# Expert weights with neighbouring rows in a partition: one 8 KB run in place of four or two rows, in a two-layer encoder with a mixture of experts

## The chip, the cores and the metric

The kernel runs on one core of a Trainium2 chip. The metric is the time of one execution on the device in microseconds (us). A profile is one execution, recorded by the hardware profiler. The engines are TensorE (PE for matmuls, PEld for its weight loads), VectorE (DVE), ScalarE (ACT), GpSimd (POOL) and SyncE (SP, which here only starts DMAs). A DMA moves data between HBM and the core's on-chip memory (SBUF); a matmul's result lies in PSUM.

## What is computed

Two layers of an encoder with 512 tokens of width 1024. Each has a mixer (attention and two kinds of linear recurrence), a mixture of 16 experts, and a gated embedding. The change touches the experts alone:

```python
h = rms_norm(x, norm_ffn_g[i])
# each token picks one of 4 groups, and 2 of the 4 experts in it, with weights comb[t, e]
for e in range(N_EXPERTS):                            # 16
    a = jax.nn.silu(t @ w_gate[e]) * (t @ w_up[e])    # [1024, 512] each
    y = y + comb[:, e:e + 1] * (a @ w_down[e])        # [512, 1024]
x = x + y
```

All of it is float32. The weights of one expert are 6 MB, those of a layer's experts 96 MB.

## The kernel before

The function `moe` computes a layer's experts one after another. On the chip a table is made of which tokens go to which expert, and the experts are ranked by how many tokens they have. The experts 0 and 1 are done first, whatever their rank; for the others the number of the expert is known only at run time, and SP reads it from SBUF (`fetch`) before it can start that expert's weight loads. In this order the first ten experts (class `Expert`, here called wide) have room for 112 rows, the last six (class `Small`, narrow) for 64. Wide experts split each weight into two parts, `hi` on ScalarE (line 244) and `lo` on VectorE (line 297), and do three matmuls for each product; narrow experts use float32 matmuls directly and do no split.

The steps for expert e are these:

- `fetch` (line 1676 and after) builds the expert's object and calls `gather` (line 1491), which clears a place in `XE` with a GpSimd memset (the first two places are filled once on ScalarE, line 1312) and gathers the expert's rows from DRAM with an indirect DMA on GpSimd's queue. `XE` has two places, used in turn, and gathers run two experts ahead.
- `scale` (line 1507) multiplies the gathered rows by the norm's gain on VectorE, in place. It is done for wide experts; narrow ones multiply by `gc`, the gain by columns, while they copy the transposed rows from PSUM (line 1605).
- `x_T` transposes the rows on TensorE in blocks of 128 columns; `x_split` copies them to SBUF.
- `gate_up(0..7)` loads the gate and up weights, 1 MB in one DMA (a block of 4 of the 8 row blocks), and does the matmuls. Row k*128 + p of a weight lies in partition p as its block k (`"(k p) n -> p k n"`), so a partition gets rows that lie 128 rows apart in DRAM.
- `silu` (ScalarE, line 1551) and `times` (VectorE, line 1554 for wide, line 1621 for narrow) make the activation `a`, 512 columns; `a_T` transposes it, `a_split` splits it.
- `down(0..3)` loads the down weights, 1 MB in one DMA (2 of the 4 row blocks), and does the matmuls. `store` (line 1591) copies the result and scatters the rows to DRAM with an indirect DMA on GpSimd's queue.

The main loop (from line 1696) weaves neighbouring experts: in the turn of e, the gate and up parts of e, the transposes of e+1, then the down parts of e-1; `store` of e-2 stands near the start. The weight loads of a layer go through a ring of 16 buffers of 1 MB (`e8`), in the order of use, on SP's queue; a load can start when the buffer's last reader is done. The tile framework puts the instructions of each engine in one fixed order at build time; `order(a, b)` asks it to keep b behind a.

Of the kernel before, what the change touches and what calls it, by code (L numbers as in the profile page):

```python
# [22 lines left out]
D = 1024  # L23
# [43 lines left out]
def tile_encoder(ctx: ExitStack, tc: tile.TileContext, A, out):  # L67
# [502 lines left out]
    def mixers(l, T_):  # L570
# [652 lines left out]
        def router_weights():  # L1223
            nonlocal wr3, wrs3, rb

            wr = small("wr", 160, bufs=1)
            wr3 = r3(wr, 8)
            nc.scalar.dma_start(wr3[:, :, 0:4], A["w_group"][l].rearrange("(k p) n -> p k n", p=128))
            nc.scalar.dma_start(wr3[:, :, 4:20], A["w_router"][l].rearrange("(k p) n -> p k n", p=128))
            gc = small("gc", 8, bufs=1)  # L1230
            nc.scalar.dma_start(gc, A["norm_ffn_g"][l].rearrange("(k p) -> p k", p=128))
            g.tensor_tensor(wr3, wr3, bc(gc.unsqueeze(2), [128, 8, 20]), OP.mult)
            st["gc"] = gc
            wrs = small("wrs", 320, F32R, bufs=1)
            wrs3 = r3(wrs, 8)
            hilo(wrs3[:, :, 0:20], wrs3[:, :, 20:40], wr3)
            rb = small("rb", 20, bufs=1)
            nc.scalar.dma_start(rb[:, 0:4], A["b_group"][l].partition_broadcast(128))
            nc.scalar.dma_start(rb[:, 4:20], A["b_router"][l].partition_broadcast(128))
# [59 lines left out]
    def moe(l, X, rsx, lg3):  # L1299
# [3 lines left out]
        st["first"], st["n"], st["h"], st["sc"] = None, 0, 0, None  # L1303
        gB = gain(A["norm_ffn_g"][l], D, "gain")

        wv_ = A["w_expert_gate"][l, 0].rearrange("(k p) n -> p k n", p=128)
        W0 = r3(t8("W0"), 4)
        nc.sync.dma_start(W0, wv_[:, 0:4, :])
        XE = t8("XE")
        i = st["last"]  # L1310
        for n in range(2):
            order(i, act(XE[:, n * D:n * D + D], bc(one_t, [128, D]), AF.Copy, scale=0.0))


        def sm4(name, n):
# [172 lines left out]

        YE = []

        def gather(ixc, n, m=CAP):
            xe = XE[0:m, (n % 2) * D:(n % 2) * D + D]
            if n > 1 or m > CAP:
                if n == 2 and Z2:
                    act(xe, bc(one_t[0:m], [m, D]), AF.Copy, scale=0.0)
                else:
                    g.memset(xe, 0.0)
            st["got"] = g.indirect_dma_start(out=xe, out_offset=None, in_=xd[:, :],
                                             in_offset=bass.IndirectOffsetOnAxis(ap=ixc[0:m], axis=0),
                                             bounds_check=T - 1, oob_is_err=False)  # L1500
            if n > G2:
                order(st["parts"], st["got"])
            if n == 2:
                st["sc"] = st["got"]
            return xe

        def scale(xe, m=CAP, after=None):
            i = v.tensor_tensor(xe, xe, gB[0:m], OP.mult)
            if after is not None:
                order(after, i)  # L1510

        class Expert:


            def __init__(self, n, w_, xe, iyc, rsc, m=CAP):
                self.n, self.w, self.xe, self.iyc, self.rsc, self.m = n, w_, xe, iyc[0:m], rsc[0:m], m
                self.rd = {}

            def x_T(self):
# [14 lines left out]
            def gate_up(self, i):  # L1534

                c, u = i // 4, i % 4
                if u == 0:
                    self.pg = mm() if c == 0 else self.pg
                    self.pu = mm() if c else None
                ps = (self.pu if c else self.pg)[0:self.m]  # L1540
                if u % 2 == 0:
                    wv_ = self.w(("w_expert_gate", "w_expert_up")[c]).rearrange("(k p) n -> p k n", p=128)
                    self.rw = W0 if self.n == c == u == 0 else load(wv_[:, 2 * u:2 * u + 4, :])
                hi, lo = split(self.rw[:, u % 2 * 2:u % 2 * 2 + 2, :], "g" if self.n == 0 and (c, u) in GS0 else "a")
                for j in range(2):
                    k = 2 * u + j
                    mm3(ps, self.xh[:, k, :], self.xl[:, k, :], hi[:, j, :], lo[:, j, :], k == 0, k == KD - 1)

            def silu(self):
                self.a = t2("a")[0:self.m]  # L1550
                act(self.a, self.pg[0:self.m], AF.Silu, scale=self.rsc)

            def times(self):
                v.tensor_tensor(self.a, self.pu[0:self.m], self.a, OP.mult)

            def a_T(self):
                self.pa = tp()
# [5 lines left out]
                self.i = hilo(self.ah, self.al, r3(self.pa, 4)[:, :, 0:self.m])  # L1563

            def load_down(self, k):
                wv_ = self.w("w_expert_down").rearrange("(k p) n -> p k n", p=128)
                raw = load(wv_[:, k:k + 2, :])
                self.rd[k], self.rd[k + 1] = raw[:, 0:1, :], raw[:, 1:2, :]

# [24 lines left out]
        class Small(Expert):  # L1594
# [7 lines left out]
            def x_split(self, q):  # L1602
                if q == 0:
                    self.x = r3(t8("xhl")[:, 0:512], 8)
                    v.tensor_tensor(self.x, r3(self.ps, 8), bc(st["gc"].unsqueeze(2), [128, 8, 64]), OP.mult)  # L1605

            def gate_up(self, k):

                if k == 0:
                    self.pg = mm()  # L1610
                if k % 4 == 0:
                    self.rw = [load(self.w(nm).rearrange("(k p) n -> p k n", p=128)[:, k:k + 4, :]) for nm in ("w_expert_gate", "w_expert_up")]
                for c in range(2):
                    pe.matmul(self.pg[64 * c:64 * c + 64], self.x[:, k, :], self.rw[c][:, k % 4, :], start=(k == 0), stop=(k == KD - 1))  # L1614

            def silu(self):
                self.a = t2("a")[64:128]
                self.si = act(self.a, self.pg[0:64], AF.Silu, scale=self.rsc)

            def times(self):  # L1620
                v.tensor_tensor(self.a, self.pg[64:128], self.a, OP.mult)

            def a_T(self):
                self.pa = tp()
# [54 lines left out]
        def fetch(e):  # L1679
# [8 lines left out]
            EX.append((Expert if e < NBIG else Small)(e, w_, gather(ic, e, m), iys[:, e:e + 1], rps[:, e:e + 1], m))  # L1688

        for e in range(GA):  # L1690
            fetch(e)
        scale(EX[0].xe)
        EX[0].x_T()
        EX[0].x_split(0)
        EX[0].x_split(1)
        for e in range(16):
            cur = EX[e]
            prev = EX[e - 1] if e else None
            if e == 15:
                s0 = turn[0]  # L1700
            fetch(e + GA)
            cur.gate_up(0)
            cur.gate_up(1)
            if e > 1:
                EX[e - 2].store()
            if e < NBIG - 1:
                scale(EX[e + 1].xe, after=st["lo"] if e else None)
            if e == 0:
                by_slot(rps, to_parts(V2, OH))
            cur.gate_up(2)  # L1710
# [2 lines left out]
            cur.gate_up(3)  # L1713
            if prev:
                prev.a_split()
            for u in range(4):
                cur.gate_up(4 + u)
                if u == (1 if e < NBIG else 3):
                    cur.silu()
                if e == 0 and u == EU:  # L1720
# [55 lines left out]
        with tc.If(cnt > 0):  # L1776
            with tc.For_i(0, 4) as r_:
# [6 lines left out]
                with tc.For_i(0, 16) as e_:  # L1784
# [3 lines left out]
                    with tc.If(ce > 0):  # L1788
# [5 lines left out]
                        ex = Expert(16, w_, gather(ic, 0, 128), jc, rc_, 128)  # L1794
                        scale(ex.xe, 128)
                        ex.x_T()
                        for q in range(2):
                            ex.x_split(q)
# [147 lines left out]
```

## Time and profile before

| what | us |
|---|---|
| median of 3 runs | 1418.15 (1415.32 to 1418.39) |
| the profiled execution | 1418.6 |
| its span, first to last instruction | 1416.9 |
| TensorE busy | 1318.4 (93%) |
| VectorE busy | 1018.7 (72%) |
| ScalarE busy | 816.7 (58%) |
| GpSimd busy | 290.7 (21%) |

304.34 MB are moved in 170,080 packets. The profile's busy time counts work that overlaps, and the end of a matmul is modelled: where TensorE's matmuls follow each other without a gap, it is read as "no idle time", not as a rate. A timeline line shows when an instruction (or a merged group of them) starts, how long it takes, its engine, line, tiles, and in brackets how long its engine was idle before and what ended that. The page's slices cut the span into 40 equal parts.

### The profile page before, as it was taken

The page shows a single profiled execution, that of the slowest core. Times are in us where ns is not written, and L with a number is a line of the kernel's source. Part 1 is how long each engine was busy: PE and PEld are TensorE (multiplying, and loading weights), DVE is VectorE, ACT ScalarE, POOL GpSimd, SP SyncE. Part 2 cuts the span into 40 slices and gives each one's busy share as a digit, 9 for nine tenths or more (in the row PEclk, how much of TensorE's full clock was granted, in tenths as well). Part 3 has the DMA queues.
Part 4 walks back from the last instruction along what each step waited for, and adds up shares of the span by engine and source line. Part 5 has one row for each costly group of instructions (what it writes and reads, how often), then busy time and mean ns, then how long its engine had stood idle before and what let it go on. Part 6 is the DMA issues. An engine that isn't in the chain of part 4 may idle for free. (4 is left out here: it accounts for less than half of the span.)

```text
span 1416.9 us, 23046 instructions
## 1 busy us (share of the span) xinstructions
PE 1318.4 (93%) x8180; PEld 1024.5 (72%) x8180; DVE 1018.7 (72%) x1931; ACT 816.7 (58%) x1565; POOL 290.7 (21%) x362
## 2 busy tenths in 40 slices
PE   6998999999899999878989989999989999998797
PEld 5787878898577775227967878789966777742296
DVE  5769887567999994118666788874779999921285
ACT  6554566554688883116555536755556888821364
POOL 4124000110344422102011330002104344221000
PEclk9999999999899999999989999999999999999999
DMA  6221224554899999998143111336358999999871
GB/s 169 80 88 49 72 60 112 187 163 162 263 376 367 369 364 365 366 379 303 35 128 91 58 46 60 79 94 226 125 208 291 382 378 371 363 358 380 318 247 60
DMA packets 170080, 304.34 MB, mean 215 GB/s; under 512 B 29216, under 2 KB 68164, under 8 KB 169956
## 3 DMA queue, kind: packets, MB, share of 16 engines
q1 hardware_dynamic: 143712, 280.00, 57.1%
q0 software_dynamic: 7872, 18.99, 4.0%
q10 hardware_dynamic: 18372, 3.79, 1.4%
q8 instruction: 67, 1.10, 0.3%
q14 instruction: 57, 0.47, 0.1%
HBM read 283.54 MB, written 20.77 MB: 215 GB/s over the span
## 5 line engine op out<-in xcount | busy, mean ns | idle before, releaser
L297 DVE TENSOR_TENSOR lo<-we,hi 128x1024 fp32r<-128x1024 f32 x236 | 276.7, 1219 | 5.9 <-ACT hi L244 2.0
L244 ACT ACTIVATE hi<-we 128x1024 fp32r<-128x1024 f32 x236 | 246.0, 1059 | 47.6 <-PE mm L335 24.6
L486 PE MATMUL zb<-hi,Th 128*128 128x256 f32 x576 | 169.4, 295 | 0.0
L487 PE MATMUL zb<-lo,Th 128*128 128x256 f32 x576 | 163.1, 283 | 0.0
L488 PE MATMUL zb<-hi,Tl 128*128 128x256 f32 x576 | 162.6, 282 | 0.0
L1591 POOL DMA_INDIRECT yd<-YE,iys x32 | 87.8, 2745 | 181.3 <-ACT YE L244 173.1
L1614 PE MATMUL mm<-we,xhl 128*64 128x512 f32 x384 | 95.7, 599 | 22.6 <-DMA we<-in_w_expert_up_dram 21.3
L486 PEld LDWEIGHTS zb<-hi,Th 128*128 128x128 f32 x576 | 109.0, 190 | 8.9 <-issue 8.0
L333 PE MATMUL mm<-hi,xhl 128*112 128x512 f32 x288 | 114.2, 398 | 0.6 <-issue 0.6
L334 PE MATMUL mm<-lo,xhl 128*112 128x512 f32 x288 | 113.6, 394 | 0.0
L335 PE MATMUL mm<-hi,xhl 128*112 128x512 f32 x288 | 113.2, 393 | 0.0
L487 PEld LDWEIGHTS zb<-lo,Th 128*128 128x128 f32 x576 | 109.3, 190 | 2.9 <-issue 1.7
L488 PEld LDWEIGHTS zb<-hi,Tl 128*128 128x128 f32 x576 | 108.9, 189 | 1.6 <-issue 1.3
L297 DVE TENSOR_TENSOR lo<-w,hi 128x1024 fp32r<-128x1024 f32 (+3 forms) x66 | 73.8, 1119 | 24.4 <-PE zb L487 18.6
L244 ACT ACTIVATE hi<-w 128x1024 fp32r<-128x1024 f32 (+3 forms) x66 | 63.0, 955 | 42.3 <-PE zb L488 35.9
L1614 PEld LDWEIGHTS mm<-we,xhl 128*64 128x64 f32 x384 | 27.6, 136 | 82.2 <-issue 43.2
L244 ACT ACTIVATE a<-mm,rps 112x512 f32<-112x512 f32 (+1 forms) x32 | 21.9, 686 | 96.1 <-PE mm L1614 78.3
L1605 DVE TENSOR_TENSOR xhl<-tp,gc 128x512 f32<-128x512 f32 x12 | 8.3, 690 | 81.5 <-PE mm L1614 55.2
L244 ACT ACTIVATE P<-mm,nm 128x512 f32<-128x512 f32 x64 | 44.1, 689 | 39.5 <-DVE nm L1016 39.2
L486 PE MATMUL zb<-hi,mh 128*128 128x256 f32 x224 | 65.0, 290 | 1.4 <-DVE X L1138 1.4
L244 ACT ACTIVATE YE<-zb 112x512 f32<-112x512 f32 (+1 forms) x62 | 34.7, 589 | 50.9 <-PE zb L1640 37.1
L333 PE MATMUL zb<-hi,ah 128*112 128x512 f32 x160 | 64.0, 402 | 0.0
(455 smaller groups left out, 3472.7 us busy)
## 6 DMA issues: line engine op xcount, KB each, us to landing
we<-in_w_expert_up_dram SPq DMA_DIRECT2D x64, 1024.0 KB, 16.8
we<-in_w_expert_down_dram SPq DMA_DIRECT2D x64, 1024.0 KB, 15.6
we<-in_w_expert_gate_dram SPq DMA_DIRECT2D x62, 1024.0 KB, 17.1
w<-in_w_in_dram SPq DMA_DIRECT2D x44, 512.0 KB, 3.8
we<-in_w_ple_gate_dram SPq DMA_DIRECT2D x8, 1024.0 KB, 13.6
Y<-yd SPq DMA_DIRECT2D x16, 512.0 KB, 9.1
X<-xd SPq DMA_DIRECT2D x12, 512.0 KB, 9.1
w<-in_w_out_dram SPq DMA_DIRECT2D x10, 512.0 KB, 3.8
```

Source lines behind the costliest of these rows:

```text
L244: i = s.activation(out_, in_, func, **kw)
L297: i = (g if eng == "g" else v).tensor_tensor(l3, src, h3.bitcast(F32), OP.subtract)
L333: i = pe.matmul(ps, ah, bh, start=start, stop=False)
L334: pe.matmul(ps, ah, bl, start=False, stop=False)
L335: return i, pe.matmul(ps, al, bh, start=False, stop=stop)
L486: pe.matmul(pt[tb], ah[c][:, sl], hi, start=(k == 0 and (by_tb or tb % 2 == 0)), stop=False, skip_group_check=True)
L487: pe.matmul(pt[tb], ah[c][:, sl], lo, start=False, stop=False, skip_group_check=True)
L488: pe.matmul(pt[tb], al[c][:, sl], hi, start=False, stop=(k == nk - 1), skip_group_check=True)
L1591: st["sc"] = g.indirect_dma_start(out=yv[self.n], out_offset=bass.IndirectOffsetOnAxis(ap=self.iyc, axis=0), in_=ye, in_offset=None, bound ...
L1605: v.tensor_tensor(self.x, r3(self.ps, 8), bc(st["gc"].unsqueeze(2), [128, 8, 64]), OP.mult)
L1614: pe.matmul(self.pg[64 * c:64 * c + 64], self.x[:, k, :], self.rw[c][:, k % 4, :], start=(k == 0), stop=(k == KD - 1))
```

## The change

The experts' weights are read with `"(p k) n -> p k n"`: partition p gets the neighbouring rows 8p to 8p+7 (gate and up, of which a load takes 4) or 4p to 4p+3 (down, of which a load takes 2), so a load's 8 KB for a partition lie in one run in DRAM. The matmuls must then meet the columns of x and of `a` in the same order: `scale` writes the gathered rows permuted into the second half of `XE`, and `silu` and `times` write `a` permuted. `XE` has one place for gathered rows and one for scaled rows; `scale` is now done for all experts, the multiplication by `gc` is gone, and the clears of gathered places are gone but for one fill at the start. In the loop the gather for e+2 stands behind `scale` of e+1.

```diff
-        wv_ = A["w_expert_gate"][l, 0].rearrange("(k p) n -> p k n", p=128)
+        wv_ = A["w_expert_gate"][l, 0].rearrange("(p k) n -> p k n", p=128)
...
-        for n in range(2):
-            order(i, act(XE[:, n * D:n * D + D], bc(one_t, [128, D]), AF.Copy, scale=0.0))
+        order(st["last"], act(XE[:, 0:D], bc(one_t, [128, D]), AF.Copy, scale=0.0))
...
         def gather(ixc, n, m=CAP):
-            xe = XE[0:m, (n % 2) * D:(n % 2) * D + D]
-            if n > 1 or m > CAP:
-                if n == 2 and Z2:
-                    act(xe, bc(one_t[0:m], [m, D]), AF.Copy, scale=0.0)
-                else:
-                    g.memset(xe, 0.0)
-            st["got"] = g.indirect_dma_start(out=xe, out_offset=None, in_=xd[:, :],
+            st["got"] = g.indirect_dma_start(out=XE[0:m, 0:D], out_offset=None, in_=xd[:, :],
...
-        def scale(xe, m=CAP, after=None):
-            i = v.tensor_tensor(xe, xe, gB[0:m], OP.mult)
+        def scale(m=CAP, after=None):
+            i = v.tensor_tensor(XE[0:m, D:2 * D].rearrange("t (k p) -> t p k", k=8), XE[0:m, 0:D].rearrange("t (p k) -> t p k", k=8),
+                                gB[0:m].rearrange("t (p k) -> t p k", k=8), OP.mult)
             if after is not None:
                 order(after, i)
 
+        def quad(ap):
+            return ap.rearrange("t (p k) -> t p k", k=4)
+
+        def by4(ap):
+            return ap.rearrange("t (k p) -> t p k", k=4)
...
-                    wv_ = self.w(("w_expert_gate", "w_expert_up")[c]).rearrange("(k p) n -> p k n", p=128)
+                    wv_ = self.w(("w_expert_gate", "w_expert_up")[c]).rearrange("(p k) n -> p k n", p=128)
...
-                act(self.a, self.pg[0:self.m], AF.Silu, scale=self.rsc)
+                act(by4(self.a), quad(self.pg[0:self.m]), AF.Silu, scale=self.rsc)
...
-                v.tensor_tensor(self.a, self.pu[0:self.m], self.a, OP.mult)
+                v.tensor_tensor(by4(self.a), quad(self.pu[0:self.m]), by4(self.a), OP.mult)
...
-                wv_ = self.w("w_expert_down").rearrange("(k p) n -> p k n", p=128)
+                wv_ = self.w("w_expert_down").rearrange("(p k) n -> p k n", p=128)
...
-                    v.tensor_tensor(self.x, r3(self.ps, 8), bc(st["gc"].unsqueeze(2), [128, 8, 64]), OP.mult)
+                    v.tensor_copy(self.x, r3(self.ps, 8))
...
-        for e in range(GA):
-            fetch(e)
-        scale(EX[0].xe)
+        fetch(0)
+        scale()
+        fetch(1)
...
-            fetch(e + GA)
             cur.gate_up(0)
             cur.gate_up(1)
             if e > 1:
                 EX[e - 2].store()
-            if e < NBIG - 1:
-                scale(EX[e + 1].xe, after=st["lo"] if e else None)
+            if 0 < e < NBIG:
+                scale(EX[e + 1].m, st["lo"])
+                fetch(e + GA)
...
             if prev:
                 prev.a_split()
+            if NBIG <= e < 15:
+                scale(CAPS, prev.i[1])
+                fetch(e + GA)
             for u in range(4):
                 cur.gate_up(4 + u)
+                if e == u == 0:
+                    scale(CAP, st["lo"])
+                    fetch(GA)
```

The narrow experts' gate and up loads, `silu` and `times` change in the same way as the wide ones'.

## Rows read from the trace of the kernel before

**Rows 1.** The page: its span, and the DMA's busy tenths in 40 slices.

```profile
span 1416.9 us, 23046 instructions
...
DMA  6221224554899999998143111336358999999871
```

**Rows 2.** Windows, layer one: start:end, length, busy PE, PEld, DVE, ACT, POOL; clock; DMA share; GB/s.

```profile
440.00:520.00 80.00, 80.00 (x385) 61.95 (x384) 77.93 (x77) 68.97 (x83) 33.16 (x14) 1.00 1.02 366
...
580.00:636.00 56.00, 43.27 (x185) 13.40 (x182) 5.07 (x9) 7.01 (x12) 4.12 (x5) 1.00 1.04 380
```

**Rows 3.** Waits in 584 to 636 us: waiter, releaser, us in total, times, longest.

```profile
PEld mm L1614 <- DMA we<-in_w_expert_up_dram: 14.0, 5, 3.1
```

**Rows 4.** TensorE's timeline: starts of narrow experts, and the ends, both layers.

```profile
556.47 2.80 PE L1614 MATMUL mm<-we,xhl 128*64 128x512 f32 x12
...
568.15 2.75 PE L1614 MATMUL mm<-we,xhl 128*64 128x512 f32 x12
...
614.54 1.07 PE L1614 MATMUL mm<-we,xhl 128*64 128x512 f32 x2 [0.22 <-DMA we<-in_w_expert_gate_dram]
...
634.04 1.94 PE L1640 MATMUL zb<-we,aT 128*64 128x512 f32 x8 [0.97 <-DMA we<-in_w_expert_down_dram]
635.91 1.09 PE L1655 MATMUL tp<-ident,p 128*128 128x128 f32 x8
...
1269.62 2.75 PE L1614 MATMUL mm<-we,xhl 128*64 128x512 f32 x12
...
1335.27 1.09 PE L1655 MATMUL tp<-ident,p 128*128 128x128 f32 x8
```

**Rows 5.** GpSimd's timeline: the scatters of two neighbouring wide experts.

```profile
455.15 5.41 POOL L1591 DMA_INDIRECT yd<-YE,iys  x1 [4.20 <-ACT YE L244]
...
472.78 5.43 POOL L1591 DMA_INDIRECT yd<-YE,iys  x1 [4.17 <-ACT YE L244]
```

**Rows 6.** Groups of VectorE by form: busy us, mean ns of one, idle before.

```profile
L1508 DVE TENSOR_TENSOR XE<-XE,gain 112x1024 f32<-112x1024 f32 x20 | 24.4, 1221 | 0.7 <-DMA XE<-xd,ix 0.7
...
L1554 DVE TENSOR_TENSOR a<-mm,a 112x512 f32<-112x512 f32 x20 | 13.6, 682 | 0.0
...
L966 DVE COPY kvs<-mm 64x256 f32<-64x256 f32 x8 | 3.3, 412 | 3.9 <-PE mm L955 3.9
...
L1630 DVE COPY aT<-tp 128x256 f32<-128x256 f32 x12 | 5.1, 425 | 28.5 <-PE tp L1626 16.1 <-issue 12.4
...
L637 DVE CAST wsh<-wst 128x256 fp32r<-128x256 f32 x2 | 1.2, 588 | 0.3 <-DMA wst<-in_w_in_dram 0.3
...
L972 DVE TENSOR_TENSOR_SCAN Ss<-db,kvs 64x512 f32<-64x512 f32 x8 | 10.1, 1266 | 0.1
```

**Rows 7.** Queue q1 in stretches of 3 us (from 1361, 1295, 333, 625): packets, MB, share.

```profile
q1 hardware_dynamic: 1036, 1.04, 109.1%
...
q1 hardware_dynamic: 573, 1.14, 104.3%
...
q1 hardware_dynamic: 328, 1.28, 104.1%
...
q1 hardware_dynamic: 286, 1.12, 102.4%
```

**Rows 8.** Head of the stage: timelines, and us to landing (360 to 400, 440 to 520).

```profile
367.31 1.01 SPq L265 DMA_DIRECT2D we<-in_w_expert_gate_dram  x2
...
371.41 1.70 POOL L1498 DMA_INDIRECT XE<-xd,ixs  x1 [2.63 <-PE mm L1407]
...
375.05 3.48 DVE L297 TENSOR_TENSOR lo<-we,hi 128x1024 fp32r<-128x1024 f32 x3
...
384.67 1.21 DVE L1508 TENSOR_TENSOR XE<-XE,gain 112x1024 f32<-112x1024 f32 x1
...
XE<-xd,ixs POOLq DMA_INDIRECT x3, 10.6
...
XE<-xd,ixs POOLq DMA_INDIRECT x4, 8.0
```

More of the change, by code (lines that the diff above doesn't have):

```diff
@@ L1232, in router_weights @@
             g.tensor_tensor(wr3, wr3, bc(gc.unsqueeze(2), [128, 8, 20]), OP.mult)
-            st["gc"] = gc
             wrs = small("wrs", 320, F32R, bufs=1)
@@ L1309, in moe @@
         XE = t8("XE")
-        i = st["last"]
-        for n in range(2):
-            order(i, act(XE[:, n * D:n * D + D], bc(one_t, [128, D]), AF.Copy, scale=0.0))
+        order(st["last"], act(XE[:, 0:D], bc(one_t, [128, D]), AF.Copy, scale=0.0))
         def sm4(name, n):
@@ L1504, in gather, with __init__ @@
                 st["sc"] = st["got"]
-            return xe
-        def scale(xe, m=CAP, after=None):
-            i = v.tensor_tensor(xe, xe, gB[0:m], OP.mult)
+        def scale(m=CAP, after=None):
+            i = v.tensor_tensor(XE[0:m, D:2 * D].rearrange("t (k p) -> t p k", k=8), XE[0:m, 0:D].rearrange("t (p k) -> t p k", k=8),
+                                gB[0:m].rearrange("t (p k) -> t p k", k=8), OP.mult)
             if after is not None:
                 order(after, i)
+        def quad(ap):
+            return ap.rearrange("t (p k) -> t p k", k=4)
+        def by4(ap):
+            return ap.rearrange("t (k p) -> t p k", k=4)
         class Expert:
-            def __init__(self, n, w_, xe, iyc, rsc, m=CAP):
-                self.n, self.w, self.xe, self.iyc, self.rsc, self.m = n, w_, xe, iyc[0:m], rsc[0:m], m
+            def __init__(self, n, w_, ixc, iyc, rsc, m=CAP):
+                self.n, self.w, self.ixc, self.iyc, self.rsc, self.m = n, w_, ixc, iyc[0:m], rsc[0:m], m
+                self.xe = XE[0:m, D:2 * D]
                 self.rd = {}
@@ L1611, in gate_up @@
                 if k % 4 == 0:
-                    self.rw = [load(self.w(nm).rearrange("(k p) n -> p k n", p=128)[:, k:k + 4, :]) for nm in ("w_expert_gate", "w_expert_up")]
+                    self.rw = [load(self.w(nm).rearrange("(p k) n -> p k n", p=128)[:, k:k + 4, :]) for nm in ("w_expert_gate", "w_expert_up")]
                 for c in range(2):
@@ L1617, in silu @@
                 self.a = t2("a")[64:128]
-                self.si = act(self.a, self.pg[0:64], AF.Silu, scale=self.rsc)
+                self.si = act(by4(self.a), quad(self.pg[0:64]), AF.Silu, scale=self.rsc)
             def times(self):
-                v.tensor_tensor(self.a, self.pg[64:128], self.a, OP.mult)
+                v.tensor_tensor(by4(self.a), quad(self.pg[64:128]), by4(self.a), OP.mult)
             def a_T(self):
@@ L1687, in fetch @@
                 w_ = lambda nm: A[nm][l][bass.DynSlice(pv, 1)].rearrange("o k n -> (o k) n")
-            EX.append((Expert if e < NBIG else Small)(e, w_, gather(ic, e, m), iys[:, e:e + 1], rps[:, e:e + 1], m))
-        for e in range(GA):
-            fetch(e)
-        scale(EX[0].xe)
+            EX.append((Expert if e < NBIG else Small)(e, w_, ic, iys[:, e:e + 1], rps[:, e:e + 1], m))
+            gather(ic, e, m)
+        fetch(0)
+        scale()
+        fetch(1)
         EX[0].x_T()
@@ L1793, in moe @@
                         w_ = lambda nm: A[nm][l][bass.DynSlice(e_, 1)].rearrange("o k n -> (o k) n")
-                        ex = Expert(16, w_, gather(ic, 0, 128), jc, rc_, 128)
-                        scale(ex.xe, 128)
+                        ex = Expert(16, w_, ic, jc, rc_, 128)
+                        gather(ic, 0, 128)
+                        scale(128)
                         ex.x_T()
```

## The prediction

> **What bounds the kernel now.** I read the page's slices first, then busy time by stage, then the timelines of TensorE, VectorE and GpSimd in the expert stage. The slices [rows 1] show two long stretches with the DMA engines full: the expert stages of the two layers, from about 367 us (the first load that needs a run-time expert number, [rows 8]) to about 636 us, and 701.5 us later again. The change lies only there.
>
> A full DMA doesn't yet say that DMA sets the end. In 440 to 520 us [rows 2] TensorE has no idle time and VectorE has 2.07 us of 80; the DMA is full because 16 buffers let it run ahead. In 580 to 636 us TensorE is idle for 12.7 of 56 us, and its waits name expert loads [rows 3]. So there are two parts: the ten wide experts run at the engines' pace and draw on the stock of buffers; when the stock is gone, in the four last narrow experts, loads set the pace.
>
> How much that costs is read from TensorE's starts [rows 4]. A narrow expert without a wait takes 568.15 - 556.47 = 11.68 us. The 16th expert would then start at 568.15 + 3 x 11.68 = 603.2 and end after 11.68 + 2 x 1.94 us, at 618.8; it ended at 635.9. In the second layer 1269.62 + 35.0 + 15.6 = 1320.2 against 1335.3. So there are 17.1 and 15.1 us that faster loads can give at most, 32 in all; beyond that the engines' chain is the end.
>
> **Part 1, the pieces.** Per partition a load now takes 4 rows of 2 KB that lie 256 KB apart (gate, up) or 2 rows of 4 KB (down); after it, 8 KB in one run. From stretches with pieces of one size [rows 7], engine time for 8 KB is share x 16 engines x 3 us / MB x 8192 B: 413 ns in 1 KB pieces, 360 ns in 2 KB, and in 4 KB 320 ns in one stretch and 360 in another. With a fixed price f per piece, 1 to 2 KB gives f = 13 ns (53/4), 2 to 4 KB gives 20 (40/2) or 0. No row shows 8 KB on this queue. I take f = 10, the middle of 0 and 20. Gate and up then save 3f = 30 ns per 8 KB, down saves 10. After 367 us a layer issues 56 gate and up loads and 28 down loads (14 experts x 6) of 128 such pieces over 16 engines: 56 x 8 x 30 + 28 x 8 x 10 ns = 15.7 us (0 to 31). The loads for the first two experts lie in stretches where the DMA has gaps, and give nothing. The loads would then allow ends at 620.2 and 1319.6.
>
> [...]
>
> **Part 2, the permuted stores on VectorE.** `scale` (112x1024, 1.22 us) and `times` (112x512, 0.68 us) [rows 6] now store each element 512 B from the one before, and `times` also reads so. VectorE's bounds: the copy at L966 reads PSUM in 512 B steps and costs 412 ns for 256 columns against 425 for a plain copy: 0 per element. The slow cast at L637 stores into SBUF in rows 512 B apart (32 words in each) and costs 588 ns for 256 columns, 163 more: 0.64 ns per element. I take 0.64, because that one hops in an SBUF store, as the change does. Then `scale` is 0.66 us longer and `times` 0.33, 0.98 us per wide expert. Per expert of 17.63 us [rows 5] VectorE is idle for 2.07/80 x 17.63 = 0.46 us [rows 2]. TensorE has no idle time and VectorE takes over as the slower: 0.98 - 0.46 + 0.2 (half of the small idle stays) = 0.72 us per expert, ten experts, 7.2 us per layer later into the narrow ones. Bounds: 0 to 15, from a scan that costs 1266 ns for 512 columns, 1.14 ns per element over `times` [rows 6]: (1.17 + 0.58 - 0.46 + 0.2) x 10.
>
> [...]
>
> **Part 3, one buffer for gathered rows.** Before, gathers ran two experts ahead in two places. Now rows are gathered into one half and scaled into the other, so the gather for expert e+2 waits for `scale` of e+1, and that waits for the transposes of e. In the steady part this has cover: from one `scale` to the next are 17.6 us, and the gather takes 5.4 us behind the scatter on GpSimd's queue [rows 5], 1.7 to issue and 8.0 to land [rows 8]: 15.1, with 2.5 us left. With narrow experts the 11.7 us hold 9.7 of issue and landing and leave 2 for the scatter. At the head the cover is thin: the gather for expert 2 was issued at 371.4 and its rows scaled at 384.7 [rows 8]; now it waits for `scale` of expert 1, which stands behind the fifth weight split (the second of the three that start at 375.1, [rows 8]) and ends near 380, and lands 10.6 us later, near 391, and VectorE, which works in order, has that `scale` in front of the weight splits. With the 0.66 us of the first `scale` I take 3 us per layer (0 to 6). Queued behind it on VectorE are the splits, and TensorE waits for them.
>
> **At no cost.** The permuted store of `silu` on ScalarE: 11 us of 80 are idle there [rows 2], 2.4 per expert, so even twice the time of one 512-column instruction is hidden; if ScalarE were full, the 0.33 us of `times` would be its cost. Narrow experts get a `scale` of 1.2 to 1.9 us; VectorE is busy for 5.07 of the last 56 us there [rows 2], and the transposes that need it come 4 us later; if it were full, the scale would stand in the chain. The narrow experts' copy in place of a product has the same 512 columns. The memsets on GpSimd and one zero fill on ScalarE go away; neither engine is the bound. The run-time expert number is now read on SP's queue after the first half of gate: it waits for nothing late after the head, and the loads that use it follow more than an expert later. At the head, the 11 loads that need no number are out before it, as now.
>
> **The sum.** Engines' chain: 618.8 + 7.2 + 3 = 629.0 and 1320.2 + 10.2 = 1330.4. Loads: 620.2 and 1319.6. The later one sets the end, so the new bound is the chain, and the loads have 9 to 11 us to spare. Gains: 635.9 - 629.0 = 6.9 and 1335.3 - 1330.4 = 4.9 us, 11.8 together. What follows each expert stage moves with it. The profiled execution took 1418.6 us, of which the span is 1416.9 [rows 1] and 1.7 lies around it, and the median of the runs is 1418.15. 1418.6 - 11.8 = **1407 us**, 1400 to 1413 for this case.
>
> **Rivals.**
> *Stores that hop are nearly free.* For it: L966. Chain 621.8 and 1323.2, loads 620.2 and 1319.6: gains 14.1 and 12.1, 1392 us. Below it lies only the 32 us of waits, 1387.
> *Pieces don't matter*, because the queue still cuts the run as before, or because the cost goes by bytes: 2 KB and 4 KB have the same 360 ns in one pair of stretches [rows 7]. Loads end as now, the longer chain (629) hides behind them: 1418 to 1419, no change.
> *VectorE pays more than the loads give: slower.* Place: `scale` and `times` of the ten wide experts. It decides from the point where chain growth passes 17.1 and 15.1 us, less the 3 at the head 1.2 to 1.4 us per expert, that is 1.5 to 1.7 us of extra VectorE work (with 0.46 - 0.2 for the idle time). At 1.14 ns per element (the scan) the chain ends at 636.7 and 1338.1: 0.8 and 2.8 us later, 1422. Against it: plain rows and hops in this trace cost at most 0.64.
> [...]
>
> **Chances.** Forecast 0.45, free hops 0.22, pieces don't matter 0.15, slower by VectorE 0.13, the head or a gather worse than bounded 0.05. A range from 1389 to 1424 takes in all but the ends of the second and the fourth. Within 0.2% (2.8 us, about what a measurement of this kernel tells from no change) falls nearly all of the third and some of the first and fourth: 0.17; slower 0.17; faster 0.66.
>
> **What would show it.** Right: no TensorE waits on loads in the last narrow experts, starts 11.7 us apart to the end; scatters of wide experts 18.2 to 18.5 us apart, VectorE without idle time, `scale` near 1.9 us and `times` near 1.0; packets of over 4 KB, some 57,000 fewer in all (of 64 gate and up and 32 down loads a layer, three of four and one of two pieces go). If scatters stay 17.6 us apart, hops are free. If waits on loads remain as long, pieces don't matter. If `scale` is over 2.4 us, the slower case. A wait of VectorE on a gather at `scale` of experts 1 or 2 shows the head. The forecast would be wrong most easily by the price of a hop, which the trace only brackets, and by gathers that land late.

## The result, and the profile after

| | before | after |
|---|---|---|
| median, us | 1417.55 (1415.32 to 1418.39) | 1435.27 (1431.96 to 1436.56) |
| the profiled execution / its span, us | 1418.6 / 1416.9 | 1434.15 / 1432.4 |
| packets in all | 170,080 | 112,736 |

The ratio is 1.0124 (95% interval 1.0102 to 1.0146): the kernel became 17.7 us slower. The prediction was 1407 us, 1389 to 1424, so it had the wrong sign.

The two expert stages hold all of it. I divide each by four events on GpSimd's queue: the first gather, the scatter of the first expert, that of the ninth, and the last. In us:

| stretch | before, layers 1 / 2 | after | forecast of the difference | measured |
|---|---|---|---|---|
| head: first gather to first scatter | 39.65 / 39.38 | 47.94 / 49.17 | +3 / +3 | +8.3 / +9.8 |
| eight wide turns: to the ninth scatter | 141.31 / 141.23 | 150.03 / 149.26 | +5.8 / +5.8 | +8.7 / +8.0 |
| narrow part: to the last scatter | 94.20 / 92.09 | 84.17 / 85.36 | -15.7 / -13.7 | -10.0 / -6.7 |

(The forecast's narrow part is what is left of its 6.9 and 4.9 us of gain.) The sum is +18.1 where -11.8 was forecast; the rest of the kernel gave 2.6 us back. No stretch came out as forecast: the gain is smaller and both losses are larger.

First the groups of the changed kernel by form, whole run (columns as in [rows 6], of which the first two are the lines of before; `silu` on ScalarE took 688 ns there):

```profile
L1501 DVE TENSOR_TENSOR XE<-XE,gain 112x1024 f32<-112x1024 f32 x20 | 40.3, 2014 | 14.9 <-DMA XE<-xd,ixs 8.6 <-DMA XE<-xd,ix 6.2
L244 ACT ACTIVATE a<-mm,rps 112x512 f32<-112x512 f32 x20 | 24.3, 1213 | 6.4 <-PE mm L335 6.4
L1501 DVE TENSOR_TENSOR XE<-XE,gain 64x1024 f32<-64x1024 f32 x12 | 23.5, 1962 | 5.0 <-DMA XE<-xd,ixs 4.8
L1555 DVE TENSOR_TENSOR a<-mm,a 112x512 f32<-112x512 f32 x20 | 21.7, 1086 | 0.9 <-PE mm L335 0.9
```

`scale` is 793 ns longer, 0.77 ns per element; `times` 404, 0.79; `silu` 525, 1.03. And `scale` now waits on gathers, 14.9 us in the wide experts of both layers.

The windows, to be held against [rows 2]: in the wide part TensorE has lost its full occupation (76.48 of 80 us), VectorE has 2.4 us left; in the narrow part TensorE is busier than before (50.26 of 56, was 43.27), since no load is late there any more.

```profile
440.00:520.00 80.00, 76.48 (x358) 57.94 (x358) 77.57 (x75) 66.20 (x78) 28.14 (x8) 1.00 1.00 366
580.00:636.00 56.00, 50.26 (x250) 17.63 (x248) 15.33 (x16) 10.50 (x13) 5.59 (x6) 0.97 1.02 395
```

The head, timelines of GpSimd and VectorE, to be held against [rows 8]. Each gather leaves only when the `scale` before it has ended, and the next `scale` waits for it at the front of VectorE's queue:

```profile
368.58 2.06 POOL L1492 DMA_INDIRECT XE<-xd,ix  x1 [2.69 <-DVE pf L1435]
...
380.98 2.78 POOL L1492 DMA_INDIRECT XE<-xd,ixs  x1 [10.33 <-DVE XE L1501]
```

and VectorE:

```profile
378.78 1.93 DVE L1501 TENSOR_TENSOR XE<-XE,gain 112x1024 f32<-112x1024 f32 x1 [2.75 <-DMA XE<-xd,ix]
...
391.28 1.91 DVE L1501 TENSOR_TENSOR XE<-XE,gain 112x1024 f32<-112x1024 f32 x1 [2.35 <-DMA XE<-xd,ixs]
```

Two wide turns, the same engines ([rows 5] are the scatters of before, 17.63 us apart). The scatters are 18.27 and 19.15 us apart:

```profile
465.75 6.57 POOL L1592 DMA_INDIRECT yd<-YE,iys  x1 [11.75 <-ACT YE L244]
472.63 1.38 POOL L1492 DMA_INDIRECT XE<-xd,ixs  x1 [0.30 <-issue]
484.02 0.97 POOL L1592 DMA_INDIRECT yd<-YE,iys  x1 [10.01 <-ACT YE L244]
486.41 5.04 POOL L1492 DMA_INDIRECT XE<-xd,ixs  x1 [1.42 <-DVE XE L1501]
503.17 6.77 POOL L1592 DMA_INDIRECT yd<-YE,iys  x1 [11.71 <-ACT YE L244]
```

and VectorE:

```profile
464.96 2.06 DVE L1501 TENSOR_TENSOR XE<-XE,gain 112x1024 f32<-112x1024 f32 x1
...
484.10 2.05 DVE L1501 TENSOR_TENSOR XE<-XE,gain 112x1024 f32<-112x1024 f32 x1 [0.58 <-DMA XE<-xd,ixs]
```

This is a closed chain. `scale` ends at 467.02; the gather for the next expert may now leave, but the scatter ahead of it on GpSimd holds the queue until 472.32; the gather starts at 472.63 and its rows let `scale` start at 484.10. From `scale` to `scale` that is 2.06 + 5.30 + 0.31 + 11.47 = 19.14 us, more than the 17.63 of a turn before. But such turns alternate with short ones without a wait (18.2 to 18.5 us), and `scale` waits only 2.1 us in all in 410 to 560 us: most of the longer turn is VectorE's longer work (e3 below).

The narrow part on TensorE: the transposes of an expert's rows wait 3.13 us for `scale`, the matmuls after it take 8.78 us where 32 of them take 7.09 elsewhere (granted clock 0.81 in 600 to 609 us, right behind that wait), and the transposes of `a` wait 0.6 to 0.7 us for `times` in three of the turns:

```profile
572.49 2.80 PE L1615 MATMUL mm<-we,xhl 128*64 128x512 f32 x12
...
599.78 0.68 PE L1601 MATMUL tp<-ident,XE 64*128 64x64 f32 x8 [3.13 <-DVE XE L1501]
600.39 8.78 PE L1615 MATMUL mm<-we,xhl 128*64 128x512 f32 x32
...
611.62 0.43 PE L1627 MATMUL tp<-ident,a 64*128 64x64 f32 x4 [0.73 <-DVE a L1622]
...
641.91 1.09 PE L1656 MATMUL tp<-ident,p 128*128 128x128 f32 x8
```

From the start that answers to 556.47 in [rows 4] the part takes 69.42 us; my unstalled count was 62.3. TensorE's waits for `scale` (3.13 and 0.70 us) and for `times` (0.73, 0.70 and 0.60) and the slower matmuls (1.69) add up to 7.6 us, so they are about the whole difference.

### The profile page after: what moved, and what is told of

It reads as the page before. It is cut to its first block, busy times and chain, and to the rows that moved or that the text cites. A ratio compares the mean times of both kernels' runs of the same rounds, so it can differ in the third digit from the quotient of the medians.

```text
span 1432.4 us, 23017 instructions
## 1 busy us (share of the span) xinstructions
PE 1325.9 (93%) x8180; PEld 1028.5 (72%) x8180; DVE 1064.9 (74%) x1943; ACT 825.2 (58%) x1561; POOL 288.5 (20%) x336
## 2 busy tenths in 40 slices
DMA packets 112736, 304.34 MB, mean 212 GB/s; under 512 B 29216, under 2 KB 68164, under 8 KB 88036
## 5 line engine op out<-in xcount | busy, mean ns | idle before, releaser
L1592 POOL DMA_INDIRECT yd<-YE,iys x32 | 81.9, 2560 | 307.7 <-ACT YE L244 295.1
L297 DVE TENSOR_TENSOR lo<-w,hi 128x1024 fp32r<-128x1024 f32 (+3 forms) x66 | 75.0, 1136 | 23.5 <-PE zb L487 18.3
L1615 PE MATMUL mm<-we,xhl 128*64 128x512 f32 x384 | 90.5, 621 | 0.0
L244 ACT ACTIVATE a<-mm,rps 112x512 f32<-112x512 f32 (+1 forms) x32 | 38.1, 1190 | 90.0 <-PE mm L1615 71.1
L1492 POOL DMA_INDIRECT XE<-xd,ixs x28 | 66.7, 2384 | 93.8 <-DVE XE L1501 90.8
L1501 DVE TENSOR_TENSOR XE<-XE,gain 112x1024 f32<-112x1024 f32 (+1 forms) x32 | 63.8, 1994 | 19.8 <-DMA XE<-xd,ixs 13.4
L334 PEld LDWEIGHTS mm<-lo,xhl 128*112 128x112 f32 x288 | 50.9, 177 | 34.0 <-DVE lo L297 19.4
```

The costliest lines, as they stand in the source:

```text
L244: i = s.activation(out_, in_, func, **kw)
L297: i = (g if eng == "g" else v).tensor_tensor(l3, src, h3.bitcast(F32), OP.subtract)
L334: pe.matmul(ps, ah, bl, start=False, stop=False)
L1492: st["got"] = g.indirect_dma_start(out=XE[0:m, 0:D], out_offset=None, in_=xd[:, :], in_offset=bass.IndirectOffsetOnAxis(ap=ixc[0:m], axis= ...
L1501: i = v.tensor_tensor(XE[0:m, D:2 * D].rearrange("t (k p) -> t p k", k=8), XE[0:m, 0:D].rearrange("t (p k) -> t p k", k=8), gB[0:m].rearra ...
L1592: st["sc"] = g.indirect_dma_start(out=yv[self.n], out_offset=bass.IndirectOffsetOnAxis(ap=self.iyc, axis=0), in_=ye, in_offset=None, bound ...
```

## The experiments

Theories: (1) *hops*, the stores that step 512 B make VectorE the bound; (2) *place*, the single place for gathered rows puts gather, `scale` and scatter into one chain; (3) *pieces*, whether 8 KB pieces bring anything at all. Where a kernel leaves the columns unmatched (e1 to e3), layer two routes tokens otherwise and takes several hundred us more; only layer one's stage, first gather to last scatter, is compared for those, but for one look at layer two in e1: 275.2 us before, 282.1 after.

**e1, the pieces alone.** Before, with

```diff
-  .rearrange("(k p) n -> p k n", p=128)
+  .rearrange("(p k) n -> p k n", p=128)
```

in the four places that read expert weights.

> The kernel before, with the weights read in 8 KB pieces and nothing else changed: no permuted stores, two places for gathered rows, no scale for narrow experts. It leaves out the matching order of the columns of x and a, so its numbers are not the reference's. If the pieces speed up the loads as the changed kernel's trace suggests (engine time for 8 KB 315 ns where 2 KB pieces took 360), the loads no longer set the end and the engines' chain of the kernel before does: stages end near 619 and 1304 to 1320, about 1386 us (1383 to 1395). If pieces don't matter, 1417 us with the same waits on loads in the last four narrow experts.

Measured: 272.4 us, a gain of 2.7 of the 17 I counted on. TensorE's timeline, then GpSimd's, show the larger part of what is missing:

```profile
624.27 0.69 PE L1626 MATMUL tp<-ident,a 64*128 64x64 f32 x4 [5.84 <-DVE a L1621]
```

and on GpSimd:

```profile
620.86 0.45 POOL L1232 TENSOR_TENSOR wr<-wr,gc 128x160 f32<-128x160 f32 x1 [25.88 <-DMA gc<-in_norm_ffn_g_dram]
```

The last expert's `silu` stands on ScalarE behind the next layer's router weights. Those need `gc`, whose one buffer the narrow experts of this layer still read. Before, the wait was hidden behind late loads. The change, which drops `gc` from the narrow experts, removes it; I hadn't counted that. The smaller part is that loads are still late: in 584 to 636 us TensorE waits 4.0 us on gate and up weights (before, 11.3 on all loads). Of these 3.5 are (columns as in [rows 3]):

```profile
PE mm L1614 <- DMA we<-in_w_expert_up_dram: 3.5, 3, 1.5
```

In layer two no next layer's router weights stand behind the experts. Its sixteen turns, the same instructions on other rows, took 262.9 us instead of 272.7, a gain of 9.8.

**e2, plain stores.** After, with `scale`, `silu` and `times` in plain order.

```diff
-            i = v.tensor_tensor(XE[0:m, D:2 * D].rearrange("t (k p) -> t p k", k=8), XE[0:m, 0:D].rearrange("t (p k) -> t p k", k=8),
-                                gB[0:m].rearrange("t (p k) -> t p k", k=8), OP.mult)
+            i = v.tensor_tensor(XE[0:m, D:2 * D], XE[0:m, 0:D], gB[0:m], OP.mult)
```

> The changed kernel with scale, silu and times reading and writing in plain order; 8 KB pieces, one place for gathered rows and one for scaled rows, and the order of the instructions stay. It leaves out the permutation, so its numbers are not the reference's. Theory 1, stores that step 512 B carry the loss: scale back to 1.22 us, times to 0.68, silu to 0.68; per layer 0.85 us x 8 wide periods, 2.4 us at the head and about 2 in the narrow experts, 11 us: 1435 - 22 = 1413 us, or lower. Theory 2, the single gather place carries it: the scale of every other expert still waits on its gather, and with a shorter turn waits longer, the head keeps its waits of 2.75 and 2.35 us: 1425 to 1432 us.

Measured: 270.3 us, 11.8 less than after. Wide turns are 17.8 us again, but the head stays at 48.5 us: that one isn't the hops'.

**e3, old pieces in the changed kernel.**

> The changed kernel with the weights read as before (2 and 4 KB pieces); permuted stores and gather places as in the change. It leaves out the matching order of the weights, so its numbers are not the reference's. If the engines' chain sets the end of the changed kernel and the pieces' gain is hidden behind it, the time stays within 4 us of 1435 us (loads of the kernel before allowed an end at 635.9 us, the changed kernel's last down matmul ends near 642). If the pieces still carry part of the time, 1440 to 1450 us with waits on loads in the narrow experts.

Measured: 279.1 us, 3.1 *less* than after. The pieces' gain is wholly hidden in the changed kernel. The wide turns are an even 18.5 us without a wait of `scale`, and gathers land sooner (median 8.9 us after the start of their issue, 410 to 560 us; 12.0 in the changed kernel, the same stretch). VectorE is idle for only 1.1 of 80 us here, so its work alone sets these turns; the changed kernel's take 18.7 to 18.8 us on average, so the chain through the gather adds 0.2 to 0.3 us a turn to that. The window of the wide part:

```profile
440.00:520.00 80.00, 77.93 (x370) 59.13 (x369) 78.90 (x76) 67.23 (x79) 33.51 (x8) 1.00 1.03 364
```

**e4 and e5, another way to match the columns.** Before, 8 KB pieces, and TensorE's transposes read in steps instead of anyone storing in steps; e5 also scales narrow rows plainly and so frees `gc`.

```diff
-                    i = pe.transpose(..., self.xe[:, kk * 128:(kk + 1) * 128],
+                    i = pe.transpose(..., self.xe.rearrange("t (p k) -> t k p", k=8)[:, kk, :],
...
-                    pe.transpose(..., self.a[:, k * 128:(k + 1) * 128], ...)
+                    pe.transpose(..., self.a.rearrange("t (p k) -> t k p", k=4)[:, k, :], ...)
...
+            if NBIG <= e < 15:
+                scale(EX[e + 1].xe, CAPS, after=prev.i[1])
```

> The kernel before with 8 KB pieces, and the columns matched where TensorE reads them: the transposes of x read every 8th column, those of a every 4th, and the gain by columns is loaded once more per layer in that order. No store steps, no extra scale, two places for gathered rows. If TensorE reads in steps of 32 and 16 B at no cost, the same time as the pieces alone, about 1386 us (1383 to 1395). If each of the 12 transposes of an expert pays 0.1 us for its steps, 1.2 us per expert on TensorE, which has no idle time in the wide experts: 38 us more, about 1424 us.

> As e4 (two places for gathered rows, 8 KB pieces, TensorE's transposes read in steps), but narrow experts get a plain scale on VectorE in place of the product with the gain by columns, so that buffer isn't read in the narrow experts. In e4's first layer the last expert's transposes waited 5.9 us for times; behind that silu stood on ScalarE behind the next layer's router weights, which waited on GpSimd for the load of that buffer. Theory: without that wait the first layer ends 6 us earlier and the second as in e4: 1403 - 6 = 1397 us (1393 to 1400). Rival: the wait only moves to the loads or to the scale: 1401 to 1405 us.

Measured: e4 1402.9 us, ratio 0.9907 (0.9888 to 0.9927); e5 **1395.2 us**, 0.9861 (0.9841 to 0.9880), 7.7 us less than e4 (6 expected). Both beat both kernels. The steps aren't free, and e4 came out between its two cases: a wide turn takes 17.9 us, and the weight loads of the transposes, by form in e5, 200 and 209 ns (141 before, without steps):

```profile
L1523 PEld LDWEIGHTS tp<-ident,XE 112*128 112x128 f32 x160 | 21.6, 200 | 4.4 <-issue 2.4
...
L1559 PEld LDWEIGHTS tp<-ident,a 112*128 112x128 f32 x80 | 12.8, 209 | 3.3 <-issue 1.6
```

**e10, the control for e5:** its plain `scale` for narrow experts, with old pieces and plain transposes.

> The kernel before with its old pieces and plain transposes; only narrow experts get a plain scale in place, and the gain by columns isn't read there any more (as in e5). Theory: the gain of e5 over the kernel before is the pieces', and the wait on the gain's buffer was hidden behind the loads of the last expert: 1416 us (1412 to 1419), with the same waits on loads in the narrow experts. Rival: most of e5's 21 us came with the scale, 1397 to 1405 us.

Measured: 1416.6 us, ratio 1.0000 (0.9985 to 1.0016). So the 21.4 us between e10 and e5 are the pieces', less TensorE's steps.

**e6, one place without hops.** e2 with e5's transposes.

> The changed kernel without its permuted accesses on VectorE and ScalarE; the columns are matched by TensorE's transposes, which read in steps. One place for gathered rows and the changed order stay. Theory, hops cost some 12 us a layer (the stage of layer one took 280.4 us in the changed kernel and 268.6 with plain stores) and the single place 8 to 9 at the head: 1435 - 24 + 4 for TensorE's steps = 1415 us (1409 to 1421), well above the kernel with two places (about 1397). Rival, the single place costs little once the hops are gone: within 4 us of that kernel, 1393 to 1401 us.

Measured: 1413.6 us, 0.9985 (0.9973 to 0.9997). Against e5, one place and its order cost 18.4 us; against the changed kernel, the hops cost 21.7. Heads, first gather and first scatter of e6, then of e5 (GpSimd): 49.06 and 41.72 us.

```profile
361.58 1.10 POOL L1492 DMA_INDIRECT XE<-xd,ix  x1 [5.81 <-DVE t L1463]
...
410.64 3.34 POOL L1592 DMA_INDIRECT yd<-YE,iys  x1 [15.29 <-ACT YE L244]
```

and e5:

```profile
359.64 1.09 POOL L1498 DMA_INDIRECT XE<-xd,ix  x1 [5.80 <-DVE t L1466]
...
401.36 3.34 POOL L1591 DMA_INDIRECT yd<-YE,iys  x1 [9.86 <-ACT YE L244]
```

**e7, hops with an early head.** After, the rows of experts 1 and 2 gathered early into a free weight buffer.

```diff
+        XG = e8("XG")
+        place = lambda n, m: XG[0:m, n * D - D:n * D] if n in (1, 2) else XE[0:m, 0:D]
...
-            st["got"] = g.indirect_dma_start(out=XE[0:m, 0:D], ...
+            st["got"] = g.indirect_dma_start(out=place(n, m), ...
```

> The changed kernel, its permuted stores kept, but the rows of experts 1 and 2 are gathered early into a free weight buffer, as far ahead as in the kernel before; from expert 3 on the single place. Theory, the head's 8.3 us come from the single place: scale of experts 1 and 2 waits for no gather, the first scatter comes 6 to 8 us earlier after the first gather, 12 to 16 us in both layers: 1421 us (1418 to 1425). Rival, the head's loss is that of the permuted stores, or is only moved to the gather of expert 3: 1432 to 1436 us.

Measured: 1413.6 us, 0.9982 (0.9970 to 0.9995), 21.7 less than after and 7 below what I expected. The heads shrink by 5.4 and 7.4 us, the stages by 8.3 and 9.5. The other 3.9 us of the two profiled executions come after the second stage, where nothing differs in the source; the mean granted clock of the whole execution was 0.981 (0.971 in the changed kernel), and why the clock differed isn't shown. In its wide part the gathers are nearly on time (`scale` waits 1.0 us in 410 to 560 us) and the turn is still 18.6 us: there too VectorE's longer work sets most of it.

**e8 and e12, other ways of the same permutation.** After, with the loops run in the result's order: stores plain, reads step. e8 does so in `scale`, `silu` and `times`; e12 only in the last two.

```diff
-            return ap.rearrange("t (p k) -> t p k", k=4)
+            return ap.rearrange("t (p k) -> t k p", k=4)
```

> The changed kernel with the same permutation, but scale, silu and times run through the result in order, so the stores are plain and the reads step: 32 B in SBUF for scale, 16 B in PSUM for silu and times. If only a store that steps is slow, scale takes 1.2 us and times 0.7, and the time is that of the changed kernel without hops less TensorE's steps: 1411 us (1407 to 1416). If a read that steps costs as much as a store, scale 2.0 us and 1433 to 1437 us.

> The changed kernel with silu and times reading PUSM in steps and storing plainly (0.69 and 0.68 us), scale as in the change (2.02 us), one place for gathered rows. e8 differs from it only in scale (2.17 us). Theory A, the wide experts go by VectorE's sum: 0.4 us less for each expert, 1427 us (1424 to 1430), and e8 lost by its longer scale. Theory B, with one place the turn is set by the gather, issued behind scale and scatter and landing late, so that VectorE's saving comes back as a longer wait of scale: 1434 to 1445 us, with the waits of scale on its gather well above the changed kernel's 8 us in layer one.

Measured: e8 1445.0 us, 1.0210 (1.0191 to 1.0229); e12 1436.9, 1.0118 (1.0074 to 1.0162; its four runs spread from 1429.5 to 1440.8). The groups of e8:

```profile
L1501 DVE TENSOR_TENSOR XE<-XE,gain 112x1024 f32<-112x1024 f32 x20 | 43.4, 2169 | 27.7 <-DMA XE<-xd,ixs 22.2 <-DMA XE<-xd,ix 5.4
L244 ACT ACTIVATE a<-mm,rps 112x512 f32<-112x512 f32 x20 | 13.8, 688 | 10.7 <-PE mm L335 10.7
L1555 DVE TENSOR_TENSOR a<-mm,a 112x512 f32<-112x512 f32 x20 | 13.7, 685 | 0.0
```

Reads of both inputs from SBUF in steps of 32 B cost `scale` even more than stepping stores (2169 against 2014 ns), the second case of the expectation, at a higher time than either case gave. Reads from PSUM in steps of 16 B cost `silu` and `times` nothing (688 and 685 ns; before, without steps, 688 and 682). Yet taking that work away made nothing faster: `scale` waits 18.3 us on gathers in layer one of e12 (360 to 645 us; 10.4 in the changed kernel). What stands ahead of a long turn of e12 (the next two scatters are 23.5 us apart), on GpSimd and VectorE:

```profile
431.71 5.49 POOL L1592 DMA_INDIRECT yd<-YE,iys  x1 [11.66 <-ACT YE L244]
437.51 7.06 POOL L1492 DMA_INDIRECT XE<-xd,ixs  x1 [0.31 <-issue]
```

and VectorE:

```profile
452.70 1.91 DVE L1501 TENSOR_TENSOR XE<-XE,gain 112x1024 f32<-112x1024 f32 x1 [3.94 <-DMA XE<-xd,ixs]
```

The gather queues behind the scatter, and lands 15.2 us after its issue began; this `scale` starts 21.7 us after the one before (430.97).

**e13 and e14, what sets e12's long turns.** e13 puts the gather ahead of the scatter on GpSimd; e14 is e12 with e7's early head.

```diff
-            if e > 1:
-                EX[e - 2].store()
             if 0 < e < NBIG:
                 scale(EX[e + 1].m, st["lo"])
                 fetch(e + GA)
+            if e > 1:
+                EX[e - 2].store()
+                if e < NBIG:
+                    order(st["got"], st["sc"])
```

> As e12 (one place for gathered rows, scale with permuted stores, silu and times stepping in PSUM), but in the wide experts' turns the gather stands before the scatter on GpSimd's queue. In e12's long turns a scatter whose issue takes 5.5 us stands ahead of the gather, the gather lands 15 us after its issue begins, and scale waits 3.9 us. Theory: the chain of scale, scatter, gather and landing sets those turns; without the scatter in it the scale's waits on its gather in layer one's wide part fall from 14 us to under 4, and the time falls from 1437 to some 1425 us (1418 to 1430). Rival: the gather's own issue is what is late, whatever stands ahead of it: waits as before, 1433 to 1440 us.

> As e7 (rows of experts 1 and 2 gathered early), with silu and times stepping in PSUM as in e12. Theory from e12, that behind a single place VectorE's saving comes back as a wait on the gather: no faster than e7's 1413.6 us, 1411 to 1422 us, with long turns of 20 us and more among the scatters. Rival, that e12's long turns were started by the late gathers of the head: 0.4 us less for each of the wide experts and about 2 us a layer in the narrow ones, 1404 us (1400 to 1408).

Measured: e13 1413.3 us, 0.9977 (0.9965 to 0.9989), 23.6 less than e12, twice what I expected; e14 1418.2, 1.0017 (1.0003 to 1.0031), no faster than e7. In e13 the gather leaves as `scale` ends, no `scale` of a wide expert waits on one after the head, and the turn is 17.9 us with the same stepping `scale` (GpSimd):

```profile
464.55 5.05 POOL L1492 DMA_INDIRECT XE<-xd,ixs  x1 [8.97 <-DVE XE L1501]
469.90 1.34 POOL L1592 DMA_INDIRECT yd<-YE,iys  x1 [0.30 <-issue]
482.48 5.05 POOL L1492 DMA_INDIRECT XE<-xd,ixs  x1 [11.24 <-DVE XE L1501]
```

So for e12 the chain through GpSimd's queue is shown, not only argued. The changed kernel itself was not run with the gather first; what the chain costs there is read from e3.

**e9 and e11, the hops of `a` alone.** e5 with plain transposes of `a`; `silu` and `times` step in PSUM (e9) or in their stores, as in the change (e11).

> As e5, but a is put in order by silu and times, which read PSUM in steps of 16 B and store plainly, and the transposes of a read plainly again; those of x keep their steps. In e8 such silu and times took 0.69 and 0.68 us, as plain ones. Theory: the 4 transposes of a per expert go back from 0.28 and 0.21 us (matmul and weight load) to 0.26 and 0.14, a third of the 12 that step; e5's 0.24 us a wide expert and some 0.6 us a narrow one shrink by a third, 2 us a layer: 1391 us (1388 to 1394). Rival, the transposes' steps were hidden: 1394 to 1397 us.

> As e9, but silu and times store a in steps of 512 B as in the change (two places for gathered rows, so no gather is late). It prices the hops of a alone. Theory: VectorE 0.40 us and ScalarE 0.53 us longer per expert; a wide expert leaves VectorE 0.5 us, so little of it shows there, and in the narrow ones, where silu and times stand in the chain, 0.7 us an expert: e9 + 3 to 6 us a layer, 1401 us (1396 to 1405). Rival, my own prediction's, that silu's steps cost nothing and VectorE has room: within 3 us of e9.

Measured: e9 1398.8 us, 0.9869 (0.9845 to 0.9894); e11 1396.2, 0.9853 (0.9828 to 0.9879). I missed both. e9's saving on TensorE was met by the loads: its last expert waits for down weights again. Its two stages are still 0.8 and 0.3 us shorter than e5's; what made it slower lies outside of them (its first gather alone came 1.6 us later), where the two kernels don't differ. TensorE's timeline of e9:

```profile
619.15 1.94 PE L1646 MATMUL zb<-we,aT 128*64 128x512 f32 x8 [0.56 <-DMA we<-in_w_expert_down_dram]
```

In e11 `silu` and `times` take 1219 and 1086 ns, and a wide turn stays at 17.8 us; TensorE has no gap in the window below: with two places the hops of `a` cost nothing in the wide turns. In the narrow ones its transposes of `a` wait 0.6 to 0.7 us for `times`, as in the changed kernel; e9 has its waits on loads there instead, and layer one's narrow part takes about the same in both (80.6 and 80.8 us from the ninth scatter to the last). The window of the wide part:

```profile
440.00:520.00 80.00, 80.00 (x383) 62.05 (x382) 78.34 (x77) 70.05 (x81) 34.96 (x13) 1.00 1.01 387
```

## Why the prediction was wrong

Three steps by medians lead from before to after: pieces, with TensorE's steps, 1416.6 to 1395.2 (e10 to e5, -21.4); one place and its order, to 1413.6 (e6, +18.4); hops in place of TensorE's steps, to 1435.3 (+21.7). By the two stages of the profiled executions alone they are -18.7, +19.1 and +19.3. In the same order the prediction had -30.8 (to 620.2 and 1320.2, the later of loads and chain), +4.6 and +14.4. The last two prices hold in this order only, since the two share limits.

Against the forecast (the table of the result) the heads lost 5.3 and 6.8 us more, the wide turns 2.9 and 2.2, and the narrow parts gave 5.7 and 7.0 us less: 30 us in all, of which the heads are 12 and the narrow parts 13.

- **Part 1, pieces: right in mechanism, too high in size.** A stretch of the changed kernel with weights alone, 612 to 615 us:

```profile
q1 hardware_dynamic: 177, 1.29, 103.3%
```

gives, by the formula of the prediction, 1.033 x 16 x 3 us / 1.29 MB x 8192 B = 315 ns for 8 KB; I had 330 for gate and up (360 less 30). Most of the packets went as forecast: 57,344, "some 57,000". So the price of a piece would be higher than I took. But the last loads, seen in e9 where they are late again, let TensorE end 11.2 us sooner after the first gather (623.42 - 361.26 against 635.91 - 362.51; 10.2 in layer two), and e1's layer two gained 9.8, not 15.7. Why the loads gained less than the stretch says isn't shown. In the changed kernel none of the gain shows (e3).
- **Part 2, hops on VectorE: right in mechanism, slightly low in size.** 0.77 and 0.79 ns per element, where I took 0.64 and bounded by 1.14. That 0.64 came so near is luck: the cast it was read from stores runs of 32 neighbouring words, so its 163 ns aren't the price of a hop at every element. Where VectorE sets the turn (e3, and nearly so e7) a wide turn grew by 0.8 and 1.0 us; I had 0.72.
- **Part 3, the steady turn: a step that failed, at a small price here.** I summed the gather's way as 5.4 + 1.7 + 8.0 = 15.1 us "with 2.5 us left"; a long turn has 19.14. I left out the chain's own `scale` (2.06 us), and landing took 11.5 us, not 8.0 as in [rows 8] (e3's median is 8.9 with old pieces, so the larger pieces are part of it). The 1.7 was even counted twice, since landing is measured from the start of the issue. I read prices from a kernel where the gather stood 5 us *ahead* of the scatter, and didn't ask what they are behind it. Because the chain binds only in every second turn, it cost the changed kernel 0.2 to 0.3 us a turn over e3, 1.3 to 2.3 us a layer. Where the chain binds more, e12 and e13 show it: with the scatter in front `scale` waits 8.1 us in 410 to 560 us, with the gather in front not at all. With a plain `scale` (e6) it waits 2.5 us, about as in the changed kernel.
- **Part 3, the head: the step that failed, 12 of the 30 us.** I gave it 3 us a layer, at most 6. One place alone costs 7.3 and 7.2 us (e6 against e5), the changed kernel lost 8.3 and 9.8. The time of the second gather I had right (landing "near 391"; `scale` at 391.28, 6.6 us later than before), but I took 3 us from it. And I had put the wait on the gather for expert 1, which now leaves only behind the first `scale`, at nothing: there are two late `scale`s (2.75 and 2.35 us of waiting at the front of VectorE's queue), and behind each stand weight splits and TensorE.
- **"At no cost": half right, and the other step that failed, 13 of the 30 us.** `silu`'s step was hidden in the wide turns where two places leave room (e11), as I said. In the narrow turns the longer `silu` and `times` weren't: the transposes of `a` waited for them. Nor was the narrow experts' `scale`: the gather has to fit between two of them (`scale` at 587.81, its gather at 590.04, the next `scale` at 597.74), and TensorE waited 3.13 us, then ran at a granted clock of 0.81. "9.7 of issue and landing", with 2 us left, again left out `scale`'s own 1.96. The narrow part took 7.1 us more than counted.
- **The chain without load waits** (618.8) was too low for the old way of scaling: in layer one a wait on `gc` stood hidden behind the loads (e1: 5.8 us; e5 against e4: 7.7). That the change drops `gc` spared the prediction this error, which is luck. A stall that goes uncovers the next, and I had looked for none but the engines' own pace.
- **The rivals.** "Slower by VectorE" had the right sign and the wrong place: VectorE's extra 1.2 us a turn cost 0.8 us of turn in e3, under the 1.2 to 1.4 that this rival needs. The right one was "the head or a gather worse than bounded", to which I had given 0.05 and no price.

## What to carry over

When a transfer moves behind work that it used to run ahead of, write its chain out as a closed loop, from an instruction's start to the same instruction's next start, with the instruction itself and everything queued ahead of the transfer, and compare it with the turn; a sum that leaves 2.5 of 17.6 us isn't cover when one of its terms was measured elsewhere. Change a layout where the reader can step cheaply (here TensorE's transposes, whose weight loads took 200 and 209 ns instead of 141, or reads from PSUM, 688 and 685 ns instead of 688 and 682) before storing in steps on the engine that has no room. Work out the first turns by themselves: there a late transfer has little to hide behind (8.3 and 9.8 us here). And when a stall is to go, look what waits behind it on every queue, not only on the bound one.

## What the runs showed of the hardware

- Reads from PSUM in steps of 16 B cost ScalarE and VectorE nothing (e8: 688 and 685 ns for 112x512, before 688 and 682), while steps of 32 B in the reads of two SBUF inputs cost VectorE 0.93 ns per element (2169 against 1221 ns for 112x1024) and steps of 512 B in `scale`'s stores 0.77 (2014). On ScalarE the stepping store is dearer, 1.03 ns per element (1213 against 688 ns for 112x512).
- A transpose that reads its weights in steps of 32 or 16 B takes 200 or 209 ns to load them (e5) instead of 141 (before).
- The issue of a gather or scatter on GpSimd took 0.89 to 0.95 us in the narrow part and 5 to 7 us in many wide turns of the changed kernel, where VectorE is busy for 97% of the time (77.57 us of 440 to 520); others in the wide turns took 1.0 to 4.8 us. Why some are long and others beside the same VectorE short isn't shown: no run here separates the causes.
